# A decoder step on one core: an MLP block's first two weight pieces split ahead of the previous block's last output group, with their second parts in the token tiles' landing places

## The chip, the cores and the metric

The kernel runs on one core of a Trainium2 chip. The time is that of the device for one execution, in microseconds, as the median of several runs. A profiled execution adds a trace: the span from its first to its last instruction, and each engine's work in it. Five engines have an instruction stream of their own and keep to its order: PE (TensorE, matrix products), DVE (VectorE), ACT (ScalarE), POOL (GpSimd) and SP, which here only issues transfers.

## The reference

One inference step of a one-layer decoder: a combined input projection, forgetting attention and an mLSTM matrix memory side by side, an output projection with layer norm, and a squared-ReLU MLP with layer norm. It is computed for a prompt of 2048 tokens and for 8 sampled sequences of 8 tokens (64 rows), whose attention goes over a paged cache of 8192 positions. All is float32. The change lies in the MLP, which for each token row x1 (1024 numbers) is

```python
hid = jnp.square(jax.nn.relu(x1 @ w1))            # w1: 1024 x 4096
return _layer_norm(DN_ALPHA * x1 + hid @ w2, ln2_g, ln2_b)   # w2: 4096 x 1024
```

## The kernel before

**Products in three passes.** A float32 operand is split into two float32r parts: the first part is the rounded copy (ACT, `split_hi`, L149), the second part the rest (DVE, `split_lo`, L152). `mm3` (L156 to L159) makes one product of three: first by first, first by second, second by first. Weights come as raw tiles `wr` (512 KB) over SP's queue; `piece` (L1142) loads one and splits it into `wh` and `wl`, each 128 x 1024.

**The MLP stage** (`phase_c`, L1282) goes over four token blocks (`CB`, L1314): three of 4 tiles with 128 tokens each, and a last one of 4 tiles and the 64 sampled rows. A block's tokens are kept turned and split in `x1h` and `x1l`, of which there is one place each. For every block the 4096 hidden columns are done in 16 groups `fc` of 256. `hidden(fc)` (L1329) takes two w1 pieces, makes for each of two halves `f` a PSUM group `ph` of 8 x 3 products over all tokens of the block, and ACT and DVE make the squared ReLU and split it into `hh` and `hl` (four places each). `output(fcs)` (L1348) takes two w2 pieces per `fc`, and for each token tile and each half of the 1024 columns adds a PSUM group `py` to the row `y` of that tile. The last call of a block takes `fc` 14 and 15 together: four w2 pieces, and each `py` group sums 4 x 3 products. After it come the layer norm of each tile (L161 to L172) and the store.

The order in the program at a boundary between blocks is: `hidden(15)`; `take_back`; `load` of the next block's tokens; `output([14, 15])`; then, in the next block, `hidden(0)`, `hidden(1)`, `output([0])` and so on.

**Token tiles.** `load` (L1315) calls, for each tile, `x1_load` (a transfer from `dx1` into a landing place) and `x1_turn` (8 transposes on PE into PSUM tiles of tag `ph`, two splits by ACT and two by DVE into `x1h` and `x1l`). The landing places are the two buffers of tag `xr` in pool `pcw`.

**Places.** Each tag has a fixed number of buffers: `wr` 4, `wh` 5, `wl` 4, `xr` 2, PSUM `ph` 3 (shared with the transposes `px`) and `py` 3. A planner at build time puts the instructions of each engine in order, in a simulated time of its own: among those that are ready, the one that comes first in the program goes first, and an instruction that writes a new tile becomes ready only when a buffer of its tag is free, that is, when the last reader of the earlier tile there is done.

**The stream beside it.** The sampled sequences' attention (`sample_attention`, L1410) is a generator whose steps are handed out by `tick` while the MLP is being written, one step per 5 us of counted work (`PACE_C`). Each step's instructions are queued behind the last one that the MLP had put on the same engine (`beside`, L114). It gathers keys and values from the cache by POOL. A pair of value tiles lies in the stream's own two buffers `vt`, and, where `vx["more"]` is set, a second pair in the landing places `xr` (`v_gather`, L1654). `vx["more"]` is cleared at `fc` 14, `take_back` at `fc` 15 runs the stream until the landing places are empty, and `load` sets it again at its end. The stream is over in the third block, at `fc` 13.

Of the kernel before, what the change touches and what calls it, by code (L numbers as in the profile page):

```python
# [11 lines left out]
F32R = mybir.dt.float32r  # L12
# [40 lines left out]
def body(ctx, tc, I, O, stages):  # L53
# [51 lines left out]
    vx = dict(more=None, live=[], next=0, of={})  # L105
# [37 lines left out]
    def bcast(src, off, n, name, pool=cst, **kw):  # L143
        t = pool.tile([128, n], F32, name=name, **kw)
        SY.dma_start(t, dap(src, off, [[0, 128], [1, n]]))
        return t

    def split_hi(dst, src, scale=1.0):
        last["ACT"] = A.activation(dst, src, AF.Copy, scale=scale)  # L149

    def split_lo(dst, src, hi, eng=None):
        r = (eng or V).tensor_tensor(dst, src, hi.bitcast(F32), op=OP.subtract)  # L152
        if eng is None:
            last["DVE"] = r
# [962 lines left out]
    pcw = es_w.enter_context(tc.tile_pool(name="pcw", bufs=1, side="right", reuse_waits="tile"))  # L1117
# [6 lines left out]
    def raw():  # L1124

        return pcw.tile([128, 1024], F32, name="wr", bufs=4)
# [12 lines left out]
    es_c = ExitStack()  # L1139
    C = {}  # L1140

    def piece(src, wr=None):  # L1142

        if wr is None:
            wr = raw().rearrange("p (k c) -> p k c", k=src.shape[1])
            SY.dma_start(wr, src)
        k = wr.shape[1]
        wh = C["pc"].tile([128, 1024], F32R, name="wh", bufs=5).rearrange("p (k c) -> p k c", k=k)
        wl = C["pc"].tile([128, 1024], F32R, name="wl", bufs=4).rearrange("p (k c) -> p k c", k=k)
        split_hi(wh, wr)  # L1150
        split_lo(wl, wr, wh)
        return wh, wl

    def row():
        return C["py"].tile([128, D], F32, name="y", bufs=5)

    def w1_pieces(fc):
        return [piece(I["w1"][0][kg * 512:kg * 512 + 512, fc * 256:fc * 256 + 256].rearrange("(k p) c -> p k c", p=128)) for kg in range(2)]

    def x1_load(t):  # L1160
        x = landing()
        n = tok_n(t)
        SY.dma_start(x[:n], dx1[tok_r(t):tok_r(t) + n])
        return x
# [117 lines left out]
    def phase_c():  # L1282
        es = ExitStack()
        pc, ph = C["pc"], es.enter_context(tc.tile_pool(name="ph", bufs=1, reuse_waits="tile"))
        ppc = es.enter_context(tc.tile_pool(name="ppc", bufs=1, space=PSUM, reuse_waits="tile"))
        w1, w2, wo = I["w1"][0], I["w2"][0], I["w_o"][0]

        def vecs(l):
            g = bcast(I[f"ln{l}_g"], 0, D, f"g{l}", pcw, tag="wr", bufs=4)
            b = bcast(I[f"ln{l}_b"], 0, D, f"b{l}", pcw, tag="wr", bufs=4)  # L1290
            return g, b

        def sampled():

            mx = pc.tile([128, 8, 64], F32, name="mxs", tag="hq", bufs=1)
            SY.dma_start(mx, dmv[:, :, S:])
            mh = ph.tile([128, 8, 64], F32R, name="mhs", tag="hh", bufs=4)
            ml = ph.tile([128, 8, 64], F32R, name="mls", tag="hl", bufs=4)
            split_hi(mh, mx)
            split_lo(ml, mx, mh)  # L1300
            y = row()
            SY.dma_start(y[:64], x_of(16))
            for c in range(4):
                ps = ppc.tile([128, 512], F32, name="py", bufs=3)[:64, :256]
                for kg in range(2):
                    wh, wl = piece(wo[kg * 512:kg * 512 + 512, c * 256:c * 256 + 256].rearrange("(k p) c -> p k c", p=128))
                    for k in range(4):
                        mm3(ps, mh[:, kg * 4 + k], ml[:, kg * 4 + k], wh[:, k], wl[:, k], kg + k == 0, kg + k == 4)
                s = slice(c * 256, c * 256 + 256)
                V.scalar_tensor_tensor(y[:64, s], y[:64, s], ALPHA, ps, op0=OP.mult, op1=OP.add)  # L1310
            layer_norm(y[:64], 64, *vecs(1), pc, "1")
            SY.dma_start(dx1[S:], y[:64])

        CB = [[0, 1, 2, 3], [4, 5, 6, 7], [8, 9, 10, 11], [12, 13, 14, 15, 16]]  # L1314
        def load(ci):  # L1315
            for i, t in enumerate(CB[ci]):
                x1_turn(t, i, x1_load(t), lambda: ppc.tile([128, 4, 128], F32, name="px2", tag="ph", bufs=3))
            vx["more"] = landing

        vx["more"] = landing  # L1320
        for ci, blk in enumerate(CB):
            W = sum(tok_n(t) for t in blk)
            off = {t: i * 128 for i, t in enumerate(blk)}
            xh, xl = C["x"]
            ys = {}
            pieces = [(0, 512)] if W == 512 else [(0, 288), (288, 576)]
            H = {}

            def hidden(fc):  # L1329
                w1p = C.pop("w1", None) or w1_pieces(fc)  # L1330
                H[fc] = []
                for f in range(2):
                    hh = ph.tile([128, 576], F32R, name="hh", bufs=4)
                    hl = ph.tile([128, 576], F32R, name="hl", bufs=4)
                    H[fc].append((hh, hl))
                    for (a, b) in pieces:
                        ps = ppc.tile([128, 512], F32, name="ph", tag="ph", bufs=3)[:, :b - a]
                        for k in range(8):
                            wh, wl = (x[:, k % 4, f * 128:(f + 1) * 128] for x in w1p[k // 4])
                            mm3(ps, wh, wl, xh[:, k, a:b], xl[:, k, a:b], k == 0, k == 7)  # L1340
                        hq = pc.tile([128, 512], F32, name="hq", tag="hq", bufs=1)[:, :b - a]
                        A.activation(hq, ps, AF.Relu)
                        A.activation(hq, hq, AF.Square)
                        split_hi(hh[:, a:b], hq)
                        split_lo(hl[:, a:b], hq, hh[:, a:b])
                        tick((b - a) * 0.01)

            def output(fcs):  # L1348
                w2p = [piece(w2[fc * 256 + k * 128:fc * 256 + k * 128 + 128].rearrange("(k p) c -> p k c", p=128)) for fc in fcs for k in range(2)]
                h = [x for fc in fcs for x in H.pop(fc)]  # L1350
                if 15 in fcs:
                    gb = vecs(2)
                for t in blk:
                    n = tok_n(t)
                    s = slice(off[t], off[t] + n)
                    if 0 in fcs:
                        ys[t] = row()
                        with tc.issue_after(last["ACT"].ins):
                            A.dma_start(ys[t][:n], dx1[tok_r(t):tok_r(t) + n])
                    for hf in range(2):  # L1360
                        cs = slice(hf * 512, (hf + 1) * 512)
                        ps = ppc.tile([128, 512], F32, name="py", bufs=3)[:n]
                        for k in range(len(h)):
                            wh, wl = (x[:, 0, cs] for x in w2p[k])
                            mm3(ps, h[k][0][:, s], h[k][1][:, s], wh, wl, k == 0, k == len(h) - 1)
                        y = ys[t][:n, cs]
                        if 15 in fcs and t == 16 and hf == 1:
                            last_norm(ys[t][:n], n, *gb, pc, ps, O["y_sample"].rearrange("b t d -> (b t) d"))
                        elif 0 in fcs:
                            V.scalar_tensor_tensor(y, y, ALPHA, ps, op0=OP.mult, op1=OP.add)  # L1370
                        else:
                            V.tensor_tensor(y, y, ps, op=OP.add)  # L1372
                        tick(1.28 * len(fcs))
                    if 15 in fcs and t < 16:
                        layer_norm(ys[t], n, *gb, pc, "2")
                        SY.dma_start(O["y_prompt"][0, t * 128:(t + 1) * 128], ys[t])

            for fc in range(16):
                if fc == 14:
                    vx["more"] = None  # L1380
                hidden(fc)
                if fc == 15 and ci < 3:
                    take_back()
                    load(ci + 1)
                if fc > 0:
                    output([14, 15] if fc == 15 else [fc - 1])
                if fc == 13 and ci == 2:
                    while acc[1] is not None:
                        tick(100.0)
                    sampled()  # L1390
        es.close()
# [415 lines left out]
```

## Time and profile before

| | before |
|---|---|
| median of 3 runs | 3389.78 us (3387.94 to 3408.33) |
| the profiled execution | 3402.92 us, its span 3401.2 us, mean granted PE clock 0.988 |
| PE busy | 3280.4 us (96%) |
| DVE busy | 2154.2 us (63%) |
| ACT busy | 1399.9 us (41%) |
| POOL busy | 892.3 us (26%) |
| moved by DMA | 646.38 MB, mean 190 GB/s |

Times in a trace count from the span's start. A timeline row has the start, the duration, the engine, the line, the operation, what it writes and reads (`out<-in`), the shapes and a count; in brackets stands how long the engine was idle before it and what ended that. Matmuls are pipelined, so their durations overlap: the distance between starts is what one costs. Rows of SP are issues of transfers, not the transfers. In a row of the windows view, after the stretch, its length and each engine's busy time (with the number of its instructions), come the granted PE clock, the DMA engines' busy share and GB/s. The MLP's first block begins near 1635 us, and the boundaries between its four blocks lie near 2043, 2498 and 2933 us.

### The profile page before, as it was taken

To read this page: it belongs to the slowest core of one execution; us is meant where nothing else is said; L and a number is where in the kernel's file an instruction comes from. 1 tells how busy PE (TensorE), PEld (TensorE's weight loads), DVE (VectorE), ACT (ScalarE), POOL (GpSimd) and SP (SyncE) were. 2 spreads that over 40 slices of the span, in tenths; PEclk is the share of its full clock that TensorE was granted. 3 is DMA by queue.
4 is the path that set the end of the run, shared out by engine and by line. 5 is a ranking of instruction groups with operands and counts; after the bars stand their busy time and mean duration, and the time that the engine had idled before them with its cause. 6 is when DMAs were issued, how large, how long until landed. Compare 5 with 4: busy or idle time off the path is not lost. (4 is left out here: it accounts for less than half of the span.)

```text
span 3401.2 us, 59499 instructions
## 1 busy us (share of the span) xinstructions
PE 3280.4 (96%) x22428; PEld 2671.8 (79%) x22428; DVE 2154.2 (63%) x5180; ACT 1399.9 (41%) x2953; POOL 892.3 (26%) x961
## 2 busy tenths in 40 slices
PE   9999999999989999999999999999999999999998
PEld 8999899888856666677777776777777777888887
DVE  5857577566468788655666658666676545644545
ACT  4434245334268888412333333232332333433332
POOL 0121233322332222276333324333233210100001
PEclk9999999999989999999999999999999999999999
DMA  5565776866653222487876768767668654532221
GB/s 167 158 193 165 219 222 202 272 218 203 224 169 82 76 79 57 166 308 240 286 269 240 241 207 305 270 222 255 223 236 312 201 175 142 169 117 87 82 80 65
DMA packets 427240, 646.38 MB, mean 190 GB/s; under 512 B 83148, under 2 KB 320016, under 8 KB 426056
## 3 DMA queue, kind: packets, MB, share of 16 engines
q1 hardware_dynamic: 350184, 363.22, 35.6%
q0 software_dynamic: 74304, 270.57, 21.6%
q10 hardware_dynamic: 2464, 8.78, 0.7%
q8 instruction: 177, 2.90, 0.4%
q14 instruction: 111, 0.91, 0.1%
HBM read 589.63 MB, written 52.83 MB: 189 GB/s over the span
## 5 line engine op out<-in xcount | busy, mean ns | idle before, releaser
L1372 DVE TENSOR_TENSOR y<-y,py 128x512 f32<-128x512 f32 (+1 forms) x475 | 320.6, 682 | 316.6 <-PE py L159 281.7
L149 ACT ACTIVATE wh<-wr 128x1024 fp32r<-128x1024 f32 x268 | 277.8, 1055 | 506.0 <-PE py L159 215.7
L159 PE MATMUL ph<-x1h,wl 128*128 128x512 f32 (+1 forms) x1280 | 452.3, 354 | 9.6 <-DVE wl L152 8.9
L157 PE MATMUL ph<-x1h,wh 128*128 128x512 f32 (+1 forms) x1280 | 454.6, 355 | 2.5 <-ACT wh L149 2.3
L158 PE MATMUL ph<-x1l,wh 128*128 128x512 f32 (+1 forms) x1280 | 453.8, 355 | 0.9 <-issue 0.9
L1547 POOL DMA_INDIRECT kT<-cache_k,idxK x256 | 267.3, 1044 | 710.1 <-PE sQ L1576 649.0
L1553 DVE STREAM_TRANSPOSE kT<-kT 128x512 f32<-128x512 f32 x512 | 330.7, 686 | 172.3 <-DMA kT<-cache_k,idxK 163.0
L157 PE MATMUL py<-wh,hh 128*128 128x512 f32 (+1 forms) x1088 | 431.8, 399 | 8.2 <-DVE y L1370 3.0
L158 PE MATMUL py<-wl,hh 128*128 128x512 f32 (+1 forms) x1088 | 426.4, 392 | 0.1
L159 PE MATMUL py<-wh,hl 128*128 128x512 f32 (+1 forms) x1088 | 426.1, 392 | 0.0
L152 DVE TENSOR_TENSOR wl<-wr,wh 128x1024 fp32r<-128x1024 f32 x268 | 334.2, 1254 | 82.0 <-ACT wh L149 27.3
L157 PE MATMUL pm<-whi,xh 128*128 128x256 f32 (+2 forms) x1088 | 317.8, 292 | 3.8 <-ACT xh L149 1.5
L158 PE MATMUL pm<-wlo,xh 128*128 128x256 f32 (+2 forms) x1088 | 311.9, 287 | 2.3 <-issue 1.3
L159 PE MATMUL pm<-whi,xl 128*128 128x256 f32 (+3 forms) x1088 | 310.5, 286 | 0.8 <-issue 0.8
L159 PEld LDWEIGHTS ph<-x1h,wl 128*128 128x128 f32 x1280 | 241.3, 189 | 45.1 <-DVE wl L152 11.1
L157 PEld LDWEIGHTS ph<-x1h,wh 128*128 128x128 f32 x1280 | 241.5, 189 | 42.2 <-issue 5.8
L158 PEld LDWEIGHTS ph<-x1l,wh 128*128 128x128 f32 x1280 | 241.4, 189 | 38.2 <-issue 5.6
L157 PEld LDWEIGHTS py<-wh,hh 128*128 128x128 f32 (+1 forms) x1088 | 200.8, 185 | 68.6 <-issue 16.2
L159 PEld LDWEIGHTS py<-wh,hl 128*128 128x128 f32 (+1 forms) x1088 | 200.9, 185 | 51.6 <-issue 4.5
L158 PEld LDWEIGHTS py<-wl,hh 128*128 128x128 f32 (+1 forms) x1088 | 201.1, 185 | 39.6 <-issue 1.3
L157 PE MATMUL pm<-xh,whi 128*128 128x256 f32 (+1 forms) x768 | 226.1, 294 | 5.9 <-ACT st L590 3.6
L159 PE MATMUL pm<-xh,wlo 128*128 128x256 f32 (+1 forms) x768 | 223.3, 291 | 0.5 <-issue 0.4
(379 smaller groups left out, 6848.4 us busy)
## 6 DMA issues: line engine op xcount, KB each, us to landing
wr<-w SPq DMA_DIRECT2D x256, 512.0 KB
wra<-w_in SPq DMA_DIRECT2D x112, 512.0 KB
Rb<-dR SPq DMA_DIRECT2D x128, 128.0 KB
qn<-dq SPq DMA_DIRECT2D x128, 64.0 KB
wr<-w_o SPq DMA_DIRECT2D x16, 512.0 KB
xr<-dmix SPq DMA_DIRECT2D x16, 512.0 KB
y<-x_prompt SPq DMA_DIRECT2D x16, 512.0 KB
dx<-y SPq DMA_DIRECT2D x16, 512.0 KB
```

What stands on the lines that cost most here:

```text
L149: last["ACT"] = A.activation(dst, src, AF.Copy, scale=scale)
L152: r = (eng or V).tensor_tensor(dst, src, hi.bitcast(F32), op=OP.subtract)
L157: T.matmul(ps, wh, xh, start=first, stop=False)
L158: T.matmul(ps, wh, xl, start=False, stop=False)
L159: last["PE"] = T.matmul(ps, wl, xh, start=False, stop=stop)
L1372: V.tensor_tensor(y, y, ps, op=OP.add)
L1547: G.indirect_dma_start(out=piece(n), out_offset=None, in_=ck, in_offset=IO(ap=idxK[:, b, j // 2, j % 2:j % 2 + 1], axis=0))
L1553: V.transpose(x, x)
```

## The change

`load`, which runs between `hidden(15)` and `output([14, 15])` of the first three blocks, now also calls `w1_pieces(0)` for the next block and keeps them in `C["w1"]`, where `hidden(0)` takes them. So the two loads, the two first-part splits and the two second-part splits stand in the program ahead of the four w2 pieces of the last output group. The two second parts don't take buffers of `wl`; they take the two landing places `xr`, after the last token tiles. `piece` and `w1_pieces` get an argument for that. The landing places are given to the value gathers again only at `fc` 1 of the next block, after `output([0])`, and no longer at the end of `load`.

```diff
-    def piece(src, wr=None):
+    def piece(src, wr=None, lo=None):
 ...
-        wl = C["pc"].tile([128, 1024], F32R, name="wl", bufs=4).rearrange("p (k c) -> p k c", k=k)
+        wl = (lo or C["pc"].tile([128, 1024], F32R, name="wl", bufs=4)).rearrange("p (k c) -> p k c", k=k)
 ...
-    def w1_pieces(fc):
-        return [piece(I["w1"][0][kg * 512:kg * 512 + 512, fc * 256:fc * 256 + 256].rearrange("(k p) c -> p k c", p=128)) for kg in range(2)]
+    def w1_pieces(fc, lo=lambda: None):
+        return [piece(I["w1"][0][kg * 512:kg * 512 + 512, fc * 256:fc * 256 + 256].rearrange("(k p) c -> p k c", p=128), None, lo())
+                for kg in range(2)]
 ...
         def load(ci):
             for i, t in enumerate(CB[ci]):
                 x1_turn(t, i, x1_load(t), lambda: ppc.tile([128, 4, 128], F32, name="px2", tag="ph", bufs=3))
-            vx["more"] = landing
+
+            C["w1"] = w1_pieces(0, lambda: pcw.tile([128, 1024], F32R, name="wlx", tag="xr", bufs=2))
 ...
                 if fc > 0:
                     output([14, 15] if fc == 15 else [fc - 1])
+                if fc == 1:
+                    vx["more"] = landing
                 if fc == 13 and ci == 2:
```

## The prediction

> **What bounds the kernel now.** I read the page's busy shares first, then the matrix engine's waits in the MLP stage (1640 us to the end), then the timelines of the places where one token block follows another. The change touches nothing before the first of them.
>
> ```profile
> span 3401.2 us, 59499 instructions
> PE 3280.4 (96%) x22428; PEld 2671.8 (79%) x22428; DVE 2154.2 (63%) x5180; ACT 1399.9 (41%) x2953; POOL 892.3 (26%) x961
> ```
>
> ```profile
> PE ph L159 <- DVE wl L152: 8.9, 4, 3.4
> PE sO L1688 <- DMA vt<-cache_v,idxV: 1.6, 1, 1.6
> PE px L1175 <- DMA xr<-dx: 0.9, 1, 0.9
> ```
>
> PE is busy 96% of the span, so a gain can only come out of its waits. In the waits view (total us, times, longest) the longest in this stage is a group's third product waiting for a second part wl: 8.9 us in four places. That is all the change can aim at: 0.3% of the span. Anything it does to the order of PE's work can cost more.
>
> The first boundary on PE, from the last product of hidden(15):
>
> ```profile
> 2043.10 1.03 PE L1175 MATMUL px<-ident,xr 128*128 128x128 f32 x8
> ...
> 2067.20 1.03 PE L1175 MATMUL px<-ident,xr 128*128 128x128 f32 x8
> ...
> 2074.52 0.39 PE L159 MATMUL py<-wh,hl 128*128 128x512 f32 x1
> 2074.75 0.39 PE L157 MATMUL ph<-x1h,wh 128*128 128x512 f32 x1
> ...
> 2079.63 0.50 PE L159 MATMUL ph<-x1h,wl 128*128 128x512 f32 x1 [3.37 <-DVE wl L152]
> ```
>
> The first and the last tile of the next block's tokens are transposed at 2043.10 and 2067.20. The last product of the output group of fc 14 and 15 starts at 2074.52, hidden(0) of the next block at 2074.75, 0.23 us later (the pitch of a 512-column product), and stops 3.37 us for wl. On DVE:
>
> ```profile
> 2076.59 2.98 DVE L152 TENSOR_TENSOR wl<-wr,wh 128x1024 fp32r<-128x1024 f32 x1
> ...
> 2079.62 1.17 DVE L152 TENSOR_TENSOR wl<-wr,wh 128x1024 fp32r<-128x1024 f32 x1
> ```
>
> These are the second parts of the next block's two w1 pieces. The four places wl are full of the output group's w2 pieces until its end, so both come too late. The change gives them other places (xr) and an earlier turn. The places wh tell how that goes:
>
> ```profile
> 2016.26 1.06 ACT L149 ACTIVATE wh<-wr 128x1024 fp32r<-128x1024 f32 x1 [1.68 <-PE ph L158]
> ...
> 2039.99 2.01 ACT L149 ACTIVATE wh<-wr 128x1024 fp32r<-128x1024 f32 x2 [15.72 <-remote]
> ...
> 2043.72 1.04 ACT L149 ACTIVATE wh<-wr 128x1024 fp32r<-128x1024 f32 x1
> ...
> 2051.02 1.06 ACT L149 ACTIVATE wh<-wr 128x1024 fp32r<-128x1024 f32 x1 [1.87 <-DMA wr<-w]
> ...
> 2072.91 1.06 ACT L149 ACTIVATE wh<-wr 128x1024 fp32r<-128x1024 f32 x1 [1.26 <-PE py L159]
> ```
>
> Counted back from hidden(0): 2072.91 and 2051.02 are its two w1 pieces; 2043.72, both of 2039.99 and 2016.26 the four w2 pieces. There are five places. The four w2 pieces and one w1 piece fill them, and the sixth first part waits for the end of the output group. That count carries the forecast.
>
> **The change, part by part.** Nothing is added or removed as arithmetic; two loads, two ACT splits and two DVE splits per boundary, at three boundaries, move ahead of the four w2 pieces.
>
> *The places wh.* Now the two w1 pieces come first. With five places, w1 takes two and w2 three; the fourth w2 piece waits until hidden(0) of the next block has read a w1 piece to the end. Every PSUM group of the output group adds up all four pieces, and there are three PSUM places py. So of its 96 products only 3 groups x 3 pieces x 3 = 27 can run before hidden(0) of the next block: 27 x 0.23 = 6.2 us. hidden(0) in turn needs the whole block's tokens loaded, transposed and split. So far that chain of token loads, two places xr deep, lies under the output group's 96 products; after the change it lies bare. Boundary 1:
>
> ```profile
> 2010.71 7.61 SPq L1146 DMA_DIRECT2D wr<-w  x4
> ...
> 2047.16 0.38 SPq L1146 DMA_DIRECT2D wr<-w  x1
> 2047.64 0.57 SPq L1163 DMA_DIRECT2D xr<-dx  x1
> 2050.63 0.38 SPq L1146 DMA_DIRECT2D wr<-w  x1
> ...
> 2055.03 0.33 SPq L1163 DMA_DIRECT2D xr<-dx  x1
> ```
>
> ```profile
> L1175 PE MATMUL px<-ident,xr 128*128 128x128 f32 x24 | 3.5, 275 | 0.0
> L1576 PE MATMUL sQ<-kT,qb 128*32 128x256 f32 x32 | 1.9, 382 | 1.3 <-DVE kT L1553 1.3
> L1688 PE MATMUL sO<-vt,PTs 128*32 128x256 f32 x16 | 1.1, 385 | 0.0
> L1645 PE MATMUL sT<-ident,S 128*128 128x128 f32 x4 | 0.6, 279 | 0.0
> ```
>
> The last token tile's load goes out at 2055.03 and its transposes run at 2067.20, the late end. An early end, estimated from B3's rows below, where a load issued at 2939.15 was transposed at 2945.59: 6.4 us, so 2061.5 here. The two w1 loads (2047.16 and 2050.63), which lie ahead of it so far, move to where w2 loads were, which speaks for the early end; w2's last two loads then take the place of the norm vectors'. With 1.0 us of transposes and about 1.3 us of splits, hidden(0) can start at 2063.8 to 2069.5, that is 20.7 to 26.4 us after 2043.10. PE has, from the grouped view of 2043 to 2064: transposes 3.5 x 32/24 = 4.7, sample attention 1.9 + 1.1 + 0.6 = 3.6, and the 6.2 us of output: 14.5 us. Later attention steps don't fill it, since each is queued behind the output product that calls it. Bare: 6.2 to 11.9 us, of which 1.3 us (the kT wait) is idle already: 4.9 to 10.6. I take 6, near the early end for the loads moved away.
>
> Boundaries 2 and 3:
>
> ```profile
> 2501.71 0.81 SPq L1163 DMA_DIRECT2D xr<-dx  x1
> ...
> 2504.49 2.17 SPq L1163 DMA_DIRECT2D xr<-dx  x1
> ```
>
> ```profile
> 2498.31 1.03 PE L1175 MATMUL px<-ident,xr 128*128 128x128 f32 x8
> ...
> 2514.26 1.06 PE L1175 MATMUL px<-ident,xr 128*128 128x128 f32 x8 [0.91 <-DMA xr<-dx]
> 2521.05 1.09 PE L1175 MATMUL px<-ident,xr 128*128 128x128 f32 x8
> ```
>
> ```profile
> 2932.65 1.03 PE L1175 MATMUL px<-ident,xr 128*128 128x128 f32 x8
> ...
> 2945.59 1.03 PE L1175 MATMUL px<-ident,xr 128*128 128x128 f32 x8
> ...
> 2951.72 0.46 PE L1175 MATMUL px<-ident,xr 64*128 64x64 f32 x4
> ...
> 2961.00 0.40 PE L159 MATMUL ph<-x1h,wl 128*128 128x288 f32 x1 [0.76 <-DVE wl L152]
> ```
>
> ```profile
> wr<-w SPq DMA_DIRECT2D x256, 512.0 KB
> ```
>
> ```profile
> 2939.15 5.06 SPq L1163 DMA_DIRECT2D xr<-dx  x2
> ```
>
> ```profile
> 2043.00:2064.00 21.00, 19.65 (x136) 15.15 (x135) 19.82 (x38) 7.50 (x13) 6.89 (x7) 1.00 0.99 369
> ...
> 2080.80:2084.20 3.40, 3.40 (x10) 2.65 (x9) 2.46 (x8) 0.00 (x0) 1.11 (x2) 0.50 0.90 275
> ...
> 2498.00:2515.00 17.00, 15.73 (x94) 12.27 (x93) 16.85 (x36) 4.95 (x9) 4.60 (x5) 1.00 0.99 354
> ```
>
> At boundary 2 PE waits for a token load that was issued 12.6 us earlier: the transfers, not the order, set the chain (DMA share 0.99 at 354 GB/s). hidden(15) ends just before 2498.31, where the first tile is turned. The last tile can't be turned before 2515.3, and is at 2521.05; with 2.3 us behind it, 19.3 to 25.0 us. PE has 4.7 + 6.2 and, as an estimate from boundary 1's rows, 1.7 of attention: 12.6. Bare 6.7 to 12.4, less 1.3 idle already (17.00 - 15.73). Taking the two w1 loads, 512 KB each, out of this stretch is worth up to 3 us at 354 GB/s: 2.4 to 11.1, and I take 5. Boundary 3 has no attention and five tiles: 2932.65 to 2951.72 and 0.8 us of splits is 19.9 us late; early, each of the chained loads at 6.4 us behind a PE with nothing else to do, about 16. PE has 5.2 + 6.2 + the first token half of hidden(0), about 1.6: 13. Bare 3 to 7; I take 4. Together +15, bounds 4.9 + 2.4 + 3 = 10.3 to 10.6 + 11.1 + 7 = 28.7.
>
> *The wait that was aimed at.* After hidden(0) the rest of the output group runs, 69 products, and holds all four wl until its end. Then hidden(1) comes, whose w1 pieces need places wl: the same wait, one piece pair later, behind the same norm work on DVE. Before, it is 3.37 us at boundary 1. I count 0; bounds -4.1 (it vanishes everywhere: 3.37 here and the 0.76 of 2961.00) to +4.1 (it doubles, since the hidden results of hidden(0) can only now be split too).
>
> *The granted clock.* In the stretch 2080.80 to 2084.20, just behind the 3.37 us idle, the windows view shows PEclk 0.50 in place of 1.00: 3.4 us at half rate, 1.7 us lost. Idle stretches of 4 to 6 us may each bring such a stretch. If two of three do, against one now: +1.7; bounds -1.7 to +3.4.
>
> The Trainium skill (TensorE: Matmul & The Clock Gate, "What's actually happening") says that PE falls to half rate after an idle window of about 3.4 us. The rows above agree, and by its rule all three boundaries would pay, which would be +3.4 in place of +1.7.
>
> *The gathers.* The landing places xr stay closed to value gathers until output(0) of the next block. The stream keeps its own pair vt; its one wait for it in this stage is 1.6 us. 0; at most a wait at each of about three steps at two boundaries, 6 x 1.6 = 9.6 us. Placing second parts in xr rather than wl costs DVE the same instruction; holding two raw places wr until the token tiles are turned only delays the norm vectors, which are needed some 20 us later: 0.
>
> *Sum.* 15 + 0 + 1.7 + 0 = +16.7 us. Against the profiled execution (3402.92 us, span 3401.2 and 1.7 around it) 3419.6; it lies 13 us above the median of its three runs, so for the median 3389.78 + 16.7 = 3406.5.
>
> **The rivals.**
>
> 1. *The aim is met.* If the fourth w2 piece gets its place before w1's second piece does, the output group runs as now and covers the chain, while one w1 piece and its second part are ready early. For it: places go by who is ready in the planner's own time, not by the trace. Against: w1 comes first in the program, and its load (four loads go out at 2010.71 to 2018.32 before) has long landed. It saves 3.37, 0.76 and the 1.7 us of clock: 3384. It is what decides if no product of hidden(0) precedes the output group's main part.
>
> 2. *The chain is bare at the late ends.* 28.7 and 3.4 of clock, with hidden(1)'s wait up by 4: about +36, 3426. For it: boundary 2 really waits for transfers. Against: fewer transfers stand ahead of the tokens.
>
> 3. *The gathers decide.* With one place, each attention step waits for its own gather; 9.6 us in place of the bare chain gives 3399, on top of it 3416. Against: before, one place is already all there is from fc 14 to the reload, without more than that one wait in the stage.
>
> Where the planner's order comes out equal to the old one in effect, nothing happens: 3390; I count that with rival 1.
>
> A rule of the Trainium skill speaks for the first rival. SBUF — State Buffer ("Who interferes with whom") says that VectorE and GpSimd lock each other out of a shared port. The second part at 2076.59 took 2.98 us against 1.17 for the next; moved away from the norm work it would save up to 1.8 us at a boundary, and 5 us in all, if it were still on PE's path.
>
> **How the numbers follow.** Forecast 0.64, own range 3396 to 3424; rival 1 with no effect 0.22; rival 2 0.08; rival 3 0.06. The range reaches from rival 1 (3384) to rival 2: 3383 to 3429. One per cent (34 us), about what a measurement of this kernel can tell from no change, is 3355.9 and 3423.7: no case reaches the lower one, 0.02; above the upper lie rival 2 and the forecast's upper tail, 0.11; within 0.87.
>
> **What would show it.** Right: hidden(0) of the next block (ph, L157) starts on PE before the bulk of the output group (py) at each boundary, with idle PE of 3 to 8 us among the token transposes and waits on DMA xr or x1h/x1l; a first part wh split only after 36 products of hidden(0); half clock behind the idle. The wl wait appears at hidden(1). Up to 2030 us both traces agree. Wrong: 96 products of py in one run ahead of hidden(0), as now, and no wl wait (rival 1); many waits of sO for vt (rival 3).

## The result, and the profile after

The changed kernel takes 3441.73 us in the median of 6 runs (3433.9 to 3454.17), the kernel before 3394.56 us (6 runs, 3387.94 to 3408.33) beside it: a ratio of 1.0133, 95% interval 1.0117 to 1.0148. The direction was forecast, the size was not: +47 us in place of +16.7, and outside the range. The two profiled executions lie closer together, spans of 3437.9 and 3401.2 us, so the traces have 36.7 us to account for.

The head of the page of the changed kernel:

```profile
span 3437.9 us, 59501 instructions
PE 3288.9 (96%) x22428; PEld 2677.8 (78%) x22428; DVE 2146.2 (62%) x5180; ACT 1400.5 (41%) x2953; POOL 889.5 (26%) x961
```

PE has the same 22428 products, and is busy 8.5 us longer with them: part of them ran at half rate. DVE, ACT and POOL have no more to do than before. The rest of the 36.7 us is idle PE. The waits view of PE in the MLP stage, after the change (total us, times, longest):

```profile
PE px L1176 <- DMA xr<-dx: 17.6, 6, 8.8
PE ph L157 <- ACT wh L149: 11.2, 3, 7.5
PE px L1176 <- DVE x1l L152: 6.2, 3, 3.8
PE sO L1692 <- DMA vt<-cache_v,idxV: 5.0, 4, 2.2
...
PE ph L159 <- DVE wl L152: 1.6, 2, 1.2
```

The wait that the change aims at is nearly gone: 8.9 us in four places before, 1.6 in two now. In its place PE waits 17.6 us for token tiles (0.9 before), and 11.2 us for first parts of weights (2.3 before). Of the 6.2 us for `x1l`, 3.8 lie at the start of the stage and are there before as well. All waits of this view add up to 61.0 us, against 34.9 before: +26.1 us.

**Boundary 1.** The timeline of PE, with the two splits of ACT that matter:

```profile
2052.11 0.40 PE L159 MATMUL py<-wh,hl 128*128 128x512 f32 x1
2061.27 1.94 PE L1176 MATMUL px<-ident,xr 128*128 128x128 f32 x8 [8.76 <-DMA xr<-dx]
2063.04 0.80 PE L157 MATMUL ph<-x1h,wh 128*128 128x512 f32 x1
...
2077.32 0.84 PE L157 MATMUL py<-wh,hh 128*128 128x512 f32 x3
...
2097.65 0.39 PE L159 MATMUL py<-wh,hl 128*128 128x512 f32 x1
2099.21 0.50 PE L159 MATMUL ph<-x1h,wl 128*128 128x512 f32 x1 [1.17 <-DVE wl L152]
```

```profile
2043.63 1.06 ACT L149 ACTIVATE wh<-wr 128x1024 fp32r<-128x1024 f32 x1
...
2074.58 1.06 ACT L149 ACTIVATE wh<-wr 128x1024 fp32r<-128x1024 f32 x1 [1.17 <-PE ph L158]
```

From the end of hidden(15) to 2052.11 exactly 27 products of the output group run. Then PE stands for 8.76 us, until the last token tile has landed. hidden(0) of the next block starts at 2063.04, and the fourth w2 piece is split only at 2074.58, released by a product of hidden(0) (`PE ph L158`): 31 us after the third. The other 69 products follow from 2077.32 to 2097.65, and then comes hidden(1), which waits 1.17 us for `wl`.

**Boundary 2.** Here the tokens' loads themselves go out late. SP's issues and PE's timeline:

```profile
2505.17 2.65 SPq L1146 DMA_DIRECT2D wr<-w  x2
2510.18 1.16 SPq L1564 DMA_DIRECT2D Rb<-dR  x2
2511.51 1.05 SPq L1164 DMA_DIRECT2D xr<-dx  x2
...
2523.59 2.81 SPq L1164 DMA_DIRECT2D xr<-dx  x2
```

```profile
2515.38 0.66 PE L1649 MATMUL sT<-ident,S 128*128 128x128 f32 x4 [0.20 <-ACT PTs L1651]
2521.59 1.97 PE L1176 MATMUL px<-ident,xr 128*128 128x128 f32 x8 [5.56 <-DMA xr<-dx]
2524.08 1.97 PE L1176 MATMUL px<-ident,xr 128*128 128x128 f32 x8 [0.52 <-DMA xr<-dx]
2527.48 1.94 PE L1176 MATMUL px<-ident,xr 128*128 128x128 f32 x8 [1.44 <-DVE x1l L152]
2530.24 1.94 PE L1176 MATMUL px<-ident,xr 128*128 128x128 f32 x8 [0.82 <-DMA xr<-dx]
2532.02 0.79 PE L157 MATMUL ph<-x1h,wh 128*128 128x512 f32 x1
...
2594.87 0.80 PE L157 MATMUL ph<-x1h,wh 128*128 128x512 f32 x1 [7.47 <-ACT wh L149]
```

All four token tiles are turned after the 27 products, not beside them. The first two loads go out at 2511.51, behind two weight loads. In the kernel before, SP's row for them stands 28 us earlier:

```profile
2483.50 1.35 SPq L1163 DMA_DIRECT2D xr<-dx  x2
```

What holds the landing places shows in the timeline of POOL. The last value tiles that it gathers into them ahead of the reload, in the changed kernel and then in the kernel before:

```profile
2498.30 0.94 POOL L1668 DMA_INDIRECT xr<-cache_v,idxV  x1 [0.30 <-DMA kT<-cache_k,idxK]
2499.54 0.94 POOL L1668 DMA_INDIRECT xr<-cache_v,idxV  x1 [0.30 <-PE py L159]
```

```profile
2442.92 1.22 POOL L1664 DMA_INDIRECT xr<-cache_v,idxV  x1 [0.27 <-POOL qb L1538]
2444.45 0.94 POOL L1664 DMA_INDIRECT xr<-cache_v,idxV  x1 [0.30 <-issue]
```

The stream's last pair takes the landing places 55 us later than before, just when the tokens want them. PE reads it only here:

```profile
2508.87 1.07 PE L1692 MATMUL sO<-xr,PTs 128*32 128x256 f32 x16
```

A likely reason is that the block began with the places closed, so that the stream's pairs come in another rhythm; what speaks for it is the run with the early reopening below. The four gaps in front of the transposes are 8.3 us. A second stall, 7.47 us, comes some 60 us later, where a weight piece for `ph` is late. ACT waits there for its raw tile:

```profile
2593.76 1.06 ACT L149 ACTIVATE wh<-wr 128x1024 fp32r<-128x1024 f32 x1 [6.63 <-DMA wr<-w]
```

**Boundary 3**, where the stream is over, has the same order (27 products, hidden(0), 69 products), and gaps of 0.6 to 2.4 us only.

**The clock.** The transposes above take 1.94 us for eight, against 1.03 before. The windows view at the stretches in which PE's clock was halved, first the changed kernel, then the kernel before (stretch, length, PE busy with the number of products, PE clock, DMA share, GB/s):

```profile
2057.30:2067.54 10.24, 6.27 (x30) 0.50 0.57 210
2234.80:2238.20 3.40, 3.40 (x11) 0.50 0.97 332
2518.10:2535.17 17.07, 10.80 (x39) 0.50 0.70 248
2589.80:2600.04 10.24, 5.17 (x12) 0.50 0.88 333
2931.10:2934.50 3.40, 3.40 (x9) 0.51 0.56 147
2978.90:2982.30 3.40, 3.40 (x16) 0.50 0.79 251
3013.10:3016.50 3.40, 3.40 (x17) 0.50 0.58 167
```

```profile
2080.80:2084.20 3.40, 3.40 (x10) 0.50 0.90 275
2162.70:2166.10 3.40, 3.40 (x32) 0.50 0.60 243
2435.80:2439.20 3.40, 3.05 (x7) 0.50 1.02 418
2562.10:2565.50 3.40, 3.40 (x12) 0.50 1.03 396
```

From boundary 1 on there were four such stretches of 3.4 us; now there are seven with 51.2 us. Busy time at half rate is twice what it would be, so they cost at most half of the 35.8 us that PE is busy in them, 17.9 us, against 6.6 before: at most +11.3. With the 26.1 us of waits that makes 37.4; from its first product to the end the MLP stage of the changed kernel is 40.0 us longer, and what lies ahead of it 3.3 us shorter.

### The profile page after: what moved, and what is told of

Its sections match the earlier page's. It is cut to its first block, busy times and chain, and to the rows that moved or that the text cites. A ratio compares the mean times of both kernels' runs of the same rounds, so it can differ in the third digit from the quotient of the medians.

```text
span 3437.9 us, 59501 instructions
## 1 busy us (share of the span) xinstructions
PE 3288.9 (96%) x22428; PEld 2677.8 (78%) x22428; DVE 2146.2 (62%) x5180; ACT 1400.5 (41%) x2953; POOL 889.5 (26%) x961
## 5 line engine op out<-in xcount | busy, mean ns | idle before, releaser
L157 PE MATMUL ph<-x1h,wh 128*128 128x512 f32 (+1 forms) x1280 | 457.8, 358 | 14.2 <-ACT wh L149 11.2
L158 PE MATMUL ph<-x1l,wh 128*128 128x512 f32 (+1 forms) x1280 | 456.9, 357 | 0.3 <-issue 0.3
L159 PE MATMUL ph<-x1h,wl 128*128 128x512 f32 (+1 forms) x1216 | 430.5, 356 | 3.5 <-DVE ln L167 1.7
L158 PE MATMUL py<-wl,hh 128*128 128x512 f32 (+1 forms) x1088 | 427.2, 393 | 0.0
L152 DVE TENSOR_TENSOR wl<-wr,wh 128x1024 fp32r<-128x1024 f32 x262 | 321.2, 1231 | 105.5 <-ACT wh L149 56.8
L158 PE MATMUL pm<-wlo,xh 128*128 128x256 f32 (+2 forms) x1088 | 311.1, 286 | 2.2 <-issue 1.4
L158 PEld LDWEIGHTS ph<-x1l,wh 128*128 128x128 f32 x1280 | 243.6, 190 | 37.4 <-issue 3.4
L159 PEld LDWEIGHTS ph<-x1h,wl 128*128 128x128 f32 x1216 | 230.3, 189 | 38.2 <-DVE wl L152 5.2
L1668 POOL DMA_INDIRECT vt<-cache_v,idxV x166 | 169.8, 1023 | 346.9 <-PE sO L1692 264.5
L158 PEld LDWEIGHTS py<-wl,hh 128*128 128x128 f32 (+1 forms) x1088 | 201.5, 185 | 41.7 <-issue 2.6
```

Source lines behind the costliest of these rows:

```text
L157: T.matmul(ps, wh, xh, start=first, stop=False)
L158: T.matmul(ps, wh, xl, start=False, stop=False)
L159: last["PE"] = T.matmul(ps, wl, xh, start=False, stop=stop)
L1668: G.indirect_dma_start(out=vt.rearrange("p f c -> p (f c)"), out_offset=None, in_=cv, in_offset=IO(ap=idxV[:, b, (kt % 4) * 4 + kt // 4, f ...
```

## The experiments

Three theories stood after the traces. *Places:* six first parts for five places `wh` bring hidden(0) ahead of the output group, so the token chain lies bare; this needs the early turn and all four w2 pieces together. *Reopening:* the landing places stay closed to the value gathers too long, or at the wrong moment (the expectations call it the gathers theory). *Transfers:* the moved loads delay the token loads. The rival to all was that any new order costs about this much. All ratios are to the kernel before on the same chip, with 95% intervals; its median was 3380 to 3398 us, by the chip, so a time in us compares only with its own. The kernels with early w1 pieces have `piece` and `w1_pieces` of the change. In the diffs below `LANDING` stands for the `lambda` of the change that gives a landing place, and `w1_piece(0, kg, LANDING)` loads and splits one of the two w1 pieces. The label in brackets is the name under which later texts refer to a run.

**One w1 piece early, the other behind the w2 pieces** (e1; one w1 piece and four w2 pieces, five first parts for five places):

```diff
-            C["w1"] = w1_pieces(0, LANDING)
+            C["w1"] = [w1_piece(0, 0, LANDING)]
 ...  # in output, behind w2p
+                if 15 in fcs and ci < 3:
+                    C["w1"].append(w1_piece(0, 1, LANDING))
```

> As the changed kernel, but only the first of the next block's two w1 pieces stands ahead of the output group of fc 14 and 15; the second stands behind its four w2 pieces (its second part still in a landing place). Then w1 and w2 together need 5 first-part places at that point, and there are 5. Places theory: no w2 piece has to wait for hidden(0), the output group covers the token loads again, PE shows no wait for DMA xr above 2 us, and the time is 3383 to 3400. Transfers theory (it is the moved loads, which delay the token loads): half of the moved loads stay moved, so about half of the 47 us stays, 3415 to 3425. Gathers theory (it is the landing places' late reopening, which is kept here): 3430 or more.

Measured: 3406.16 us, 1.0029 (1.0016 to 1.0043). One piece fewer takes most of the loss away. All 96 output products run ahead of hidden(0) again at boundary 1, as the places theory has it, but the time is 6 us above its range and the longest token wait is 2.5 us and not under 2. The late reopening, which this kernel keeps and which has a cost of its own in the runs below, can account for that.

**Both w1 pieces behind the w2 pieces** (e2), their second parts still in the landing places, the late reopening kept:

```diff
-            C["w1"] = w1_pieces(0, LANDING)      # in load
 ...  # in output, behind w2p
+                if 15 in fcs and ci < 3:
+                    C["w1"] = w1_pieces(0, LANDING)
```

> As the changed kernel, but both w1 pieces stand behind the four w2 pieces, as in the kernel before; their second parts still go to the landing places, which still reopen for gathers at fc 1. Places theory: 3383 to 3400, and what is left of the wait of hidden(0) for second parts is under 2 us at each boundary, since wl is no longer short. Transfers theory: the loads are in the old order, so 3385 to 3400 too. Gathers theory: 3430 or more.

Measured: 3406.9 us, 1.0034 (1.0018 to 1.005). The early turn is undone, and the loss falls from 1.33% to 0.34%, not to nothing; that lies between the ranges of all the theories.

**The last output group cut in two**, so that its first half needs two w2 pieces only; once with the change (e3), once in the kernel before as its control (e8):

```diff
-                    output([14, 15] if fc == 15 else [fc - 1])
+                    for g in ([[14], [15]] if ci < 3 else [[14, 15]]) if fc == 15 else [[fc - 1]]:
+                        output(g)
```

> As the changed kernel, but in the first three blocks the output group of fc 14 and 15 is cut in two, first 14 and then 15, each with two w2 pieces; it adds 8 row additions of 0.68 us per block on DVE, beside PE's work. The moved loads, the landing places and the late reopening stay. Places theory: output of 14 needs only two w2 pieces, so 48 products come free ahead of hidden(0) instead of 27 and nothing hangs on the fourth piece: 3392 to 3408. Transfers theory: 3430 or more. Gathers theory: 3430 or more.

> The kernel before with its last output group of the first three blocks cut in two, as in e3, and nothing of the change. If the cut by itself is a gain (the places wh and wl come free 24 products earlier), 3380 to 3390, and e3's level owes to it and not to the change. If it is neutral, 3392 to 3402, and the moved pieces are what bought e3 back its 16 us of late reopening.

Measured: with the change 3393.09 us, 0.9987 (0.9973 to 1.0001); without it 3383.53 us, 1.0012 (0.9998 to 1.0026). The cut is worth nothing by itself. With it, the same early turn and the same late reopening cost nothing that can be told from zero. So the order of the pieces hurts where one product group needs all four of them. That the late reopening is free here and not elsewhere isn't explained by this.

**The late reopening alone** (e4), in the kernel before:

```diff
-            vx["more"] = landing                 # end of load
 ...
+                if fc == 1:
+                    vx["more"] = landing
```

> As the kernel before, with one part of the change: the landing places are given to the value gathers again only at fc 1 of the next block. Places and transfers theories: within 0.3% of before, 3385 to 3405. Gathers theory: 3415 to 3440, with more than 10 us of PE waiting for gathered values (vt).

Measured: 3414.03 us, 1.005 (1.0034 to 1.0067). The part that the prediction priced at 0 costs half a per cent by itself. The sign that the gathers theory named is missing, though: PE waits 4.9 us for `vt`, not more than 10.

**The change with the early reopening** (e5; `vx["more"] = landing` back at the end of `load`):

> The changed kernel with one part undone: the landing places are given back to the value gathers at the end of the load, as in the kernel before, and no longer at fc 1. If the late reopening costs the changed kernel what it cost by itself (0.5%, 16 us), 3425. If the bare token chain has swallowed it, since the gathers then have more time, 3437 to 3445, no different from the changed kernel. If gathers queue behind hidden(0) for the landing places and hold up POOL's queue, 3445 or more.

Measured: 3406.26 us, 1.0076 (1.0053 to 1.01). That is the early turn alone. With the change's 1.0133, the late reopening is worth 0.57% in it, close to the 0.50% of the run before. PE's wait for tokens at boundary 2 is 2.7 us here.

**Cut and early reopening together** (e9):

> e3 (the changed kernel with its last output group cut in two) and e5's undoing together: nothing waits for hidden(0), and the landing places go back to the value gathers at the end of the load. If both costs are gone and the w1 pieces' early turn is worth what the old wait of hidden(0) was, ratio to before 0.990 to 0.997. If the gathers now wait for the landing places until hidden(0) has read the second parts and the stream loses by it, 1.000 to 1.006.

Measured: 3381.55 us, 1.0004 (0.9992 to 1.0016): the early turn's 0.76% is gone with the cut, but no gain is left from it either. The waits views show where it went. The early reopening without the cut, then with it:

```profile
PE px L1176 <- DMA xr<-dx: 14.3, 4, 9.0
PE ph L157 <- ACT wh L149: 9.3, 3, 4.8
```

```profile
PE ph L157 <- ACT wh L149: 6.6, 2, 5.4
...
PE px L1176 <- DMA xr<-dx: 4.6, 3, 2.1
```

The wait for token tiles falls from 14.3 to 4.6 us with nothing done to the tokens' loads: more of the output products lie over them again.

**Both w1 pieces behind the w2 pieces, and the landing places open again right behind them** (e10):

```diff
-            C["w1"] = w1_pieces(0, LANDING)      # in load
 ...
-                if fc == 1:
-                    vx["more"] = landing
 ...  # in output, behind w2p
+                if 15 in fcs and ci < 3:
+                    C["w1"] = w1_pieces(0, LANDING)
+                    vx["more"] = landing
```

> e2 (both w1 pieces behind the four w2 pieces, second parts in the landing places) with the landing places given back behind them and not at fc 1. If e2's 0.34% is the late reopening (0.5% by itself), the ratio is 0.996 to 1.000; if it is the second parts in xr, it stays at 1.002 to 1.005.

Measured: 3371.88 us against 3381.79, 0.9977 (0.9965 to 0.9988): faster than both kernels. Its waits:

```profile
PE sO L1692 <- DMA vt<-cache_v,idxV: 5.4, 3, 2.5
...
PE ph L157 <- ACT wh L149: 2.1, 1, 2.1
PE px L1176 <- DMA xr<-dx: 1.9, 1, 1.9
```

No wait of a hidden group for a second part `wl` is left, and the one for tokens is 1.9 us (0.9 before). So the second parts in the landing places, with the w1 pieces behind the w2 pieces and the places open again at once, gain a little; the earlier turn and the late reopening are what cost. Nor is a new order a loss by itself: e3, e9 and this kernel have one and lose nothing. How much of the gain is due to the places alone isn't separated: by the program the two w1 loads now also stand ahead of the norm's vectors, where before they stood behind them. The run without its early reopening (e2, 1.0034) is 0.57% slower, about the same figure a third time.

**How long the landing places stay closed**, in the kernel before: reopened at `fc` 5 (e12), and right after the last output group has been written (e13), in place of `fc` 1:

```diff
+                if fc == 5:                      # or: if fc == 15 and ci < 3
+                    vx["more"] = landing
```

> The kernel before with the landing places closed to value gathers until fc 5 of the next block, where e4 has fc 1. Lead theory (a value step waits for its own gather as long as the second pair of places is closed): four more groups of about 27 us closed at two boundaries, cost 1.0 to 2.0% and 25 us or more of PE waiting for vt. Order theory (the closing only shifts which work the planner puts where, and a few waits of other kinds come out differently): 0 to 0.7%, and not above e4's 0.5% by more than its interval.

> The kernel before with the landing places closed only until the output group of fc 14 and 15 has been handed out, which is some 30 us of program less than e4. Lead theory: 0.1 to 0.25%. Order theory: anything between -0.2 and 0.6%.

Measured: 3412.06 us, 1.0046 (1.0031 to 1.006), and 3412.78 us, 1.0043 (1.0026 to 1.0059). With `fc` 1's 1.005 these are three equal prices for three lengths. So it isn't the number of attention steps that must do with one pair. All that the three closings share in the program is that the places are closed while the last output group is being written. Both ratios lie where the order theory put them and outside the lead theory's ranges. The waits view of the longest closing shows what little the gathers themselves wait:

```profile
PE sO L1689 <- DMA vt<-cache_v,idxV: 6.4, 7, 2.2
...
PE px L1175 <- DMA xr<-dx: 2.8, 3, 1.3
```

6.4 us against 1.6, so less than a third of the 15.7 us. With `fc` 1 and `fc` 5 the rhythm shifts as in the changed kernel: a pair is gathered into the landing places at 2483 and at 2497, and the token loads follow at 2496 and 2507. But with the shortest closing the last pair lies at 2443 and the loads go out at 2484, as before, and it costs as much; there PE waits for the third tile:

```profile
2514.46 1.94 PE L1175 MATMUL px<-ident,xr 128*128 128x128 f32 x8 [6.22 <-DMA xr<-dx]
```

So the late pair is one way to the loss, not the whole of it; what the three have in common, beyond a token wait and a stretch of half rate (6.8 us each) at boundary 2, stays open. That a new order of work costs this much, whatever the gathers do, isn't ruled out. Nor is the price the same everywhere: beside the cut output group the late reopening cost nothing (e3 with it 0.9987, e9 without 1.0004).

**Only two token tiles loaded per block** (e6). The third and later tiles of a block are turned from the first two, so part of the tokens is left out and the chain of loads is short:

```diff
+            two = [x1_load(t) for t in CB[ci][:2]]
             for i, t in enumerate(CB[ci]):
-                x1_turn(t, i, x1_load(t), ...)
+                x1_turn(t, i, two[i % 2], ...)
```

> The changed kernel without the token loads from the third tile of a block on: the later tiles are turned from the copies of the first two, so a part of the tokens is left out of the result. Chain theory (PE's idle time ahead of hidden(0) is the chain of token loads through two places): the idle time in front of the transposes of the third tile on goes, 15 to 25 us less than the changed kernel, 3417 to 3427, and what is left is late first tiles and the time after the output group. Splits theory (the transposes and splits themselves are bare): at most 5 us less, 3437 to 3442.

Measured: 3411.43 us, 1.0101 (1.0076 to 1.0127). That is 0.3%, some 11 us, less than the change, where 15 to 25 were expected. Its waits go some way to say why:

```profile
PE px L1176 <- DMA xr<-dx: 5.8, 2, 5.4
```

The 8.8 us at boundary 1 are gone; at boundary 2 the first two tiles are late (5.4 us), and these it still loads.

**The norm's vectors left out in the first three blocks** (scale and shift come from a constant in place of a load), which frees raw places `wr` and the queue at the boundary; with the change (e7), and in the kernel before as control (e11):

```diff
-                    gb = vecs(2)
+                    gb = vecs(2) if ci == 3 else (None, None)
```

> The changed kernel without the loads of the second norm's two vectors in the first three blocks (the identity matrix stands in for them, so this part of the norm is left out). Raw-place theory (the vectors hold two of the four raw weight places until the last tile's norm, which now comes 15 us later against hidden(1), so the w1 and w2 loads behind the output group come late; the 7.9 us of PE idle near 2587 is of this kind): that idle time goes, with its half clock 8 to 14 us less, 3428 to 3434. Otherwise, if the loads are late for the transfers' own sake, the saving is the 3 MB of loads, at most 3 us.

> Control to e7: the kernel before without the loads of the second norm's two vectors in its first three blocks (the identity matrix in their place, that part of the norm left out). Raw-place theory: there the vectors' places come free before they are needed, so at most 0.1% is gained, against 0.29% from the changed kernel. If the gain is 0.3% here as well, the vectors' loads cost both kernels the same and explain nothing of the difference.

Measured: with the change 3413.0 us, 1.0104 (1.008 to 1.0128), which is 0.29% less than the change has; in the kernel before 3375.73 us, 0.9979 (0.9966 to 0.9992), which is 0.21% less. With the change the waits for `wh` shrink from 11.2 us to:

```profile
PE ph L157 <- ACT wh L149: 1.9, 1, 1.9
```

The 7.47 us stall is gone, but the waits for tokens are 19.7 us in place of 17.6, and the time falls hardly more than in the control. Whether holding the raw places costs anything can't be told from these two.

## Why the prediction was wrong

Two steps of the prediction failed: it put the late reopening of the landing places at 0, and it took too little for what the early turn brings with it, most of all for the clock. The step it rests on, the count of places, was right.

**Right: the mechanism of the early turn, to the product.** Six first parts for five places, 27 products ahead of hidden(0), the fourth w2 piece behind hidden(0)'s reading, 69 products after it, tokens in the open. The runs confirm the cause as well as the order: with one piece fewer early the loss falls to 0.29%, reopening included, and with an output group that doesn't need all four pieces it is gone (1.0076 without the cut, 1.0004 with it, both with the early reopening). The first rival needed the output group in one run ahead of hidden(0); it wasn't.

**Right in its bounds, in part by luck: the bare chain.** Boundary 1: forecast +6, bounds 4.9 to 10.6; measured 8.8 in the one gap and 0.4 in another. Boundary 2: +5, bounds 2.4 to 11.1; 8.3 in four gaps, but for another reason than the forecast's, since the token loads went out late; with the early reopening PE waits 2.7 us for tokens there. Boundary 3: +4, measured 3.1 for tiles and their splits. So about 21 us where I took 15, in bounds of 10.3 to 28.7. What failed in it is the choice of the early end at boundary 1. I took 6.4 us from issue to use, from boundary 3; the load issued at 2048.70, 6.3 us earlier than before, was used at 2061.27, 12.6 us after. The trace had that figure, quoted for boundary 2, in a stretch as full of transfers. At boundary 3 the stream is over and gathers nothing; at boundary 1 its gathers share the DMA engines with the token load (last section). Moving two weight loads elsewhere didn't shorten it.

**Failed: "the gathers 0, at most 9.6".** The reopening costs 0.50% (about 17 us) alone and 0.57% (about 19 us) in the change. I priced it as steps that wait for their own gathers; the test of the length shows that this isn't the price. What the trace shows is one way to the loss: at boundary 2 of the changed kernel the last pair of values holds the landing places when the tokens want them, and the token loads go out 28 us later, behind weight loads. With the early reopening they go out at 2467.13, 15 us ahead of the block's first transpose, as in the kernel before (2483.50 and 2498.31). The shortest closing costs as much without such a shift, so the full cause of this cost stays open. What was missed for sure is the other use of the closed places: the prediction looked at the attention steps and not at the token loads that want the same two buffers.

**Failed: the clock, "+1.7".** I counted one stretch of 3.4 us at each of two boundaries, against one before. The three long stretches are 10.2, 17.1 and 10.2 us, and all seven cost up to 11.3 us more than before. In each of the three, half rate began while PE still waited, and lasted until 6.3, 4.9 and 5.2 us after the end of the last gap (2061.27 to 2067.54, 2530.24 to 2535.17, 2594.87 to 2600.04). The Trainium skill (TensorE: Matmul & The Clock Gate, "What's actually happening") says that the full clock comes back after a window of about 3.4 us of sustained work, and that the windows run on freely. The lengths 10.24 and 17.07 agree: they are three and five times 3.41.

**Failed the other way: the aimed-at wait, "0 (-4.1 to +4.1)".** It fell from 8.9 to 1.6 us, more than the bound, since I counted two of its four places; the others, 2.72 us at 2560.99 and 2.00 us at 2993.89, were in later hidden groups. The wait for `wh` rose at the same time (2.3 to 11.2), but 7.47 us of it is the stall in which ACT itself waited for its raw tile.

**Open: "holding two raw places: 0".** The stall of 7.47 us looked like the price, but the control gains nearly as much. The hold is there in the trace: at boundary 1 SP, before it can issue the next weight load, waits 11.5 us for the raw place of a w1 piece, whose second part waits for the last token tile.

```profile
SPq L1146 <- DVE wlx L152: 11.5, 1, 11.5
```

What that costs, no run shows by itself.

The terms as the trace has them: 21 for the chain, up to 11 for the clock, 7.5 for the second stall, less 7.3 for the aimed-at wait, which is some 32 of the 36.7 us. By the experiments the same loss is 0.76% (26 us) for the early turn and 0.57% (19 us) for the reopening, of the 45 us by which the medians' ratio stands above 1. The forecast had 16.7 us for the early turn and nothing for the reopening. The profile before could not price the reopening; but its upper bound was drawn from one kind of wait alone, and that made the range too narrow.

## What to carry to other kernels

Before a piece is moved ahead in a list of places, count the places against everything that one product group needs together: the piece that falls out at the end decides, not the one moved in. Giving an operand a place of its own (here the second parts in the landing places) and moving it earlier are two changes; the first with the pieces left behind the group gained 0.23%, both together (with the places open again in time) lost 0.76%. A switch that only closes a buffer pair to another stream is a change of its own: here it cost about 0.5%, and it takes a run by itself to see it.

## What the runs showed of the hardware

A halved PE clock lasted 10.24 us at single gaps of 8.76 and 7.47 us, and 17.07 us where four gaps of 5.56, 0.52, 1.44 and 0.82 us stood between short transposes. In the kernel before, gaps of 3.37, 2.72, 1.65 and 0.81 us had a stretch of 3.41 us beside them, and one of 2.00 us (2993.89) none; so the length of a gap alone doesn't tell. A 512 KB load into a full DMA system was used 12.6 us after its issue, when it ended PE's wait, at boundary 1 after the change as at boundary 2 before, though at the former two weight loads had been taken out from in front of it. The stretch between that load's issue and its use, in the windows view after the change:

```profile
2048.70:2061.30 12.60, 3.47 (x20) 0.84 0.98 353
```

PE is busy for 3.47 of the 12.60 us, and the DMA engines are at 0.98 of their time. Of the 4.45 MB moved in it, 2.63 went over the software queue, which I take for that of POOL's gathers (packets, MB, share of the engines' time):

```profile
q0 software_dynamic: 736, 2.63, 59.1%
```
